# Sliding windows of a 4-D tensor: part of the input goes through the store buffers on its way in

## The chip, the cores and the metric

The kernel runs on one core of a Trainium2 chip. The metric is the device time of one execution in microseconds (us). The five engines that appear below are TensorE (PE, unused here), VectorE (DVE), ScalarE (ACT), GpSimd (POOL) and SyncE (SP). DMAs can be issued from SP, ScalarE and POOL; each of these has a DMA queue of its own (q1, q10 and q0 in the profile), and all queues are served by the same 16 DMA engines.

## The reference

The input x is 16 batches x 64 channels x 64 x 64, float32. All windows of 8 x 8 at stride 4 are copied out; nothing is computed.

```
n_h = (h - window_size) // stride + 1      # 15
n_w = (w - window_size) // stride + 1      # 15
for i in range(n_h):
    for j in range(n_w):
        result[:, i, j] = x[:, :, i*4 : i*4 + 8, j*4 : j*4 + 8]
```

The output is 16 x 15 x 15 x 64 x 8 x 8 float32, 59.0 MB; the input is 16.8 MB.

## The kernel before

The whole input is loaded once into a tile `L` of 128 partitions. The image's rows are cut into four quarters of 16 rows (`HQ`), the channels into two halves of 32 (`CH`, `CL`). Partition `ch * 64 + b * 4 + q` holds channel half `ch`, batch `b` and row quarter `q`; along the partition lie 32 channels of 16 rows of 64 numbers, so that one channel is a run of 4 KB in HBM and in `L`. The batches come in two groups of eight, `y` = 0 and 1; a group is 32 consecutive partitions in each channel half.

Loads are made by `load(eng, ch, y, q, c0, c1)`: one row quarter of the eight batches of a group, channels c0 to c1 of one half. It touches eight partitions, each four apart. The loop over y and q issues, for each pair, channels 4 to 32 of half 0 from SP (the first five pairs in two DMAs of 14 channels, the other three in one of 28), channels 0 to 4 of half 0 from POOL and channels 0 to 32 of half 1 from POOL. One DMA ahead of the loop, from ScalarE, loads channels 0 to 8 (`EC`) of half 1 for row quarter 0 and all 16 batches; POOL's loads for q = 0 leave these out. Each DMA has one of eight semaphores of its kind (eight for SP and ScalarE together, eight for POOL), so that the ninth DMA of a kind waits until the first has landed.

A store buffer is a tile `G0` to `G3` of 128 partitions x 4096 numbers; a partition holds one window of one batch with its 64 channels, 16 KB, which is one row of the output. VectorE and ScalarE fill a buffer out of `L` with copies and shuffles, and POOL writes it out with one indirect DMA (`scatter`, recorded at L131), the row numbers being in small index tiles (`idx`, `idx_y`, `idx_lo`, `idx_hi`). The last two buffers are written by SP. The four buffers are used in turn.

Three kinds of buffers follow each other. `part(y, j)` uses one batch group only: it fills four groups of 32 partitions with two window rows and two window columns, eight copies of 32 x 2048, three on ScalarE and five on VectorE (recorded at L189). `unit(j, s)` uses all batches and fills two halves of 64 partitions (L151, L154, L161, L165). The first three buffers are parts of group 0, which need only the loads of that group; then parts of group 1 alternate with units; then units alone. Two special buffers with the last window column end the program (L236).

The order of instructions on each engine is set by the framework: it schedules the program as written by the readiness of its operands, so that a ready copy can pass one that still waits for a load. It also sets all waits, from the partitions and columns of a tile that an instruction reads and writes.

Of the kernel before, what the change touches and what calls it, by code (L numbers as in the profile page):

```python
# [10 lines left out]
def kernel(  # L11
# [7 lines left out]
    nc = tc.nc  # L19
    P = nc.NUM_PARTITIONS  # L20

    B, C, H, W = x.shape
    Bo, NH, NW, Co, WSo, WSo2 = out.shape
    WS = int(window_size)
# [3 lines left out]
    f32 = mybir.dt.float32  # L28
    i32 = mybir.dt.int32
    ALU = mybir.AluOpType  # L30
    CH = 2
    HQ = P // (B * CH)
    CL = C // CH
    RB = H // HQ
# [3 lines left out]
    HP = P // CH  # L38
    YB = 8
    NY = B // YB  # L40
    QP = YB * HQ
# [4 lines left out]
    gpool = ctx.enter_context(tc.tile_pool(name="gpool", bufs=1))  # L46


    L = lpool.tile([P, CL, RB, W], f32)
# [1 line left out]

    SMALL, HWP, TWICE = 4, 8, 5

    def load(eng, ch, y, q, c0, c1):
        p0 = ch * HP + y * QP + q
        eng.dma_start(out=L[p0 : p0 + QP - HQ + 1 : HQ, c0:c1, :, :], in_=x_v[ch, y, q, :, c0:c1, :])  # L58
# [42 lines left out]
    tt(idx_lo, idx_lo, th, ALU.add)  # L101


    EC = 8
    x_b = x.rearrange("b (ch cl) (hq r) w -> ch hq b cl (r w)", ch=CH, hq=HQ)
    nc.scalar.dma_start(out=L[HP : HP + (B - 1) * HQ + 1 : HQ, 0:EC, :, :], in_=x_b[1, 0, :, 0:EC, :])

    for y in range(NY):
        for q in range(HQ):
            hw = y * HQ + q < HWP  # L110
            if hw:
                mid = (SMALL + CL) // 2 if y * HQ + q < TWICE else CL
                load(nc.sync, 0, y, q, SMALL, mid)
                if mid < CL:
                    load(nc.sync, 0, y, q, mid, CL)
            load(nc.gpsimd, 0, y, q, 0, SMALL if hw else CL)
            load(nc.gpsimd, 1, y, q, EC if q == 0 else 0, CL)

    o_v = out.rearrange("b i j c r w -> (b i j) (c r w)")
    nxt = [min(p + 1, 31) for p in range(32)]  # L120
    NG = 4
    G = [gpool.tile([P, C, WS, WS], f32, name=f"G{n}") for n in range(NG)]

    o_q = out.rearrange("b i j c r w -> i j b (c r w)")

    def free(st):
# [50 lines left out]
    def tile_():  # L177
        nonlocal at
        at += 1
        return G[(at - 1) % NG]  # L180

# [46 lines left out]
    for s in range(2):  # L228
        g = tile_()
        cols = slice(j * ST, j * ST + WS)  # L230
        for y in range(NY):
            d = slice(QP + y * QP, QP + (y + 1) * QP)
            for ch in range(CH):
                f = slice(ch * HP + y * QP, ch * HP + (y + 1) * QP)
# [39 lines left out]
```

## Time and profile before

| | |
|---|---|
| median of 3 runs | 188.5 us (188.49 to 189.4) |
| the profiled execution | 189.08 us, of which the profile's span is 187.3 us |
| VectorE, ScalarE, POOL busy | 76%, 74%, 24% of the span |
| DMA | 75.81 MB at 405 GB/s in the mean |
| HBM | 16.78 MB read, 62.91 MB written |
| POOL's queue q0 | 65.81 MB, loads and scatters |
| SP's queue q1 | 9.44 MB, 13 loads and the last two stores |
| ScalarE's queue q10 | 0.52 MB, one load |

The profile divides the span into 40 slices of 4.68 us. A DMA's share is the mean busy share of the 16 DMA engines. In the timeline a row gives the start, the time taken, the engine, the line, the operation, the tiles written and read, and in brackets how long the engine had been idle and what ended that. In part 5 of the page a copy of 32 partitions x 2048 numbers takes 1896 ns on ScalarE and 1224 ns on VectorE; the copies of L236 with 768 numbers on ScalarE take 830 ns and those with 1280 on VectorE 818 ns. A later load waits for an earlier one in the timeline as POOL's `DMA_DIRECT2D` with `DMA L<-in_x_dram` in brackets.

### The profile page before, as it was taken

The page shows a single profiled execution, that of the slowest core. Times are in us where ns is not written, and L with a number is a line of the kernel's source. Part 1 is how long each engine was busy: PE and PEld are TensorE (multiplying, and loading weights), DVE is VectorE, ACT ScalarE, POOL GpSimd, SP SyncE. Part 2 cuts the span into 40 slices and gives each one's busy share as a digit, 9 for nine tenths or more (in the row PEclk, how much of TensorE's full clock was granted, in tenths as well). Part 3 has the DMA queues.
Part 4 walks back from the last instruction along what each step waited for, and adds up shares of the span by engine and source line. Part 5 has one row for each costly group of instructions (what it writes and reads, how often), then busy time and mean ns, then how long its engine had stood idle before and what let it go on. Part 6 is the DMA issues. An engine that isn't in the chain of part 4 may idle for free.

```text
span 187.3 us, 567 instructions
## 1 busy us (share of the span) xinstructions
DVE 142.5 (76%) x203; ACT 139.3 (74%) x94; POOL 45.0 (24%) x50
## 2 busy tenths in 40 slices
DVE  5000009998597969799999999999999999999600
ACT  0000009998599979988899999998999899989700
POOL 7411222207207050501222222112211121113000
DMA  5999999999999999999999999999999999999994
GB/s 127 295 402 400 400 400 398 399 400 419 421 427 437 425 427 423 441 413 434 434 420 432 422 434 413 441 430 420 434 416 436 406 437 409 420 423 406 441 420 206
DMA packets 10988, 75.81 MB, mean 405 GB/s; under 512 B 3288, under 2 KB 3288, under 8 KB 7384
## 3 DMA queue, kind: packets, MB, share of 16 engines
q0 software_dynamic: 8784, 65.81, 84.6%
q1 hardware_dynamic: 2056, 9.44, 12.8%
q10 hardware_dynamic: 144, 0.52, 1.1%
q14 instruction: 4, 0.03, 0.0%
HBM read 16.78 MB, written 62.91 MB: 425 GB/s over the span
## 4 chain that ended last, share of the span: by engine, by line
DMA 53%; DVE 28%; issue 6%; ACT 5%; POOL 2%; ACTq 1%; DVEq 0%; PEldq 0%
DMA L<-in_x_dram 20%; DMA out_dram<-G,idx_y 14%; DVE G L161 14%; DMA out_dram<-G,idx 13%; DVE G L154 9%; DMA out_dram<-G,idx_lo 6%; DVE G L189 4%; ACT G L236 3%; POOL L L58 2%; ACT G L151 1%; ACT G L165 1%; ACTq L269 1%; DVE G L151 0%; POOL pi L69 0%; DVEq L161 0%
## 5 line engine op out<-in xcount | busy, mean ns | idle before, releaser
L151 ACT COPY G<-L 64x2048 f32<-64x2048 f32 x46 | 87.2, 1896 | 5.1 <-DMA out_dram<-G,idx 2.9
L189 DVE COPY G<-L 32x2048 f32<-32x2048 f32 x30 | 36.7, 1224 | 29.9 <-DMA L<-in_x_dram 24.1
L161 DVE STREAM_SHUFFLE G<-L 64x1024 f32<-64x1024 f32 (+4 forms) x39 | 53.0, 1360 | 1.3
L154 DVE STREAM_SHUFFLE G<-L 64x1024 f32<-64x1024 f32 x30 | 38.4, 1281 | 0.0
L189 ACT COPY G<-L 32x2048 f32<-32x2048 f32 x18 | 33.9, 1896 | 4.1 <-DMA L<-in_x_dram 2.8
L189 ACT ACT_TABLE_LOAD x1 | 1.3, 1283 | 27.7 <-DMA L<-in_x_dram 27.7
L131 POOL DMA_INDIRECT out_dram<-G,idx_y x6 | 10.0, 1664 | 28.4 <-DVE G L189 27.4
L58 POOL DMA_DIRECT2D L<-in_x_dram x16 | 11.0, 700 | 22.2 <-DMA L<-in_x_dram 21.7
L131 POOL DMA_INDIRECT out_dram<-G,idx_lo x8 | 7.7, 961 | 30.6 <-DVE G L154 26.9
L131 POOL DMA_INDIRECT out_dram<-G,idx x8 | 9.2, 1152 | 17.8 <-DVE G L161 6.8
L131 POOL DMA_INDIRECT out_dram<-G,idx_hi x7 | 6.7, 960 | 27.0 <-DVE G L154 19.0
L165 ACT COPY G<-L 64x256 f32<-64x256 f32 (+2 forms) x21 | 10.2, 484 | 0.5
L151 DVE COPY G<-L 64x2048 f32<-64x2048 f32 x6 | 7.3, 1222 | 0.2
L236 ACT COPY G<-L 32x768 f32<-32x768 f32 x8 | 6.6, 830 | 0.1
L236 DVE COPY G<-L 32x1280 f32<-32x1280 f32 x8 | 6.5, 818 | 0.1
L161 DVE LOAD_MASK_SELECT G<-L x39 | 0.3, 9 | 1.2 <-DMA out_dram<-G,idx_y 0.9
L72 DVE TENSOR_SCALAR tb<-pi 128x1 int32<-128x1 int32 x1 | 0.2, 155 | 1.0 <-POOL pi L69 1.0
L166 DVE COPY G<-L 64x1280 f32<-64x1280 f32 x1 | 0.9, 876 | 0.0
L78 DVE TENSOR_TENSOR th<-tc,tq 128x1 int32<-128x1 int32 x2 | 0.3, 156 | 0.0
L75 DVE TENSOR_SCALAR th<-tc 128x1 int32<-128x1 int32 x2 | 0.3, 154 | 0.0
L69 POOL IOTA pi<- 128x1 int32 x1 | 0.1, 124 | 0.4 <-PEq L269 0.4
L78 DVE CUSTOM_DVE_ANT_0 idx<-tb,th 128x2 uint16<-128x2 uint16 x1 | 0.2, 160 | 0.0
(19 smaller groups left out, 2.7 us busy)
## 6 DMA issues: line engine op xcount, KB each, us to landing
L<-in_x_dram POOLq DMA_DIRECT2D x6, 1024.0 KB, 21.6
L<-in_x_dram SPq DMA_DIRECT2D x10, 448.0 KB
L<-in_x_dram SPq DMA_DIRECT2D x3, 896.0 KB
out_dram<-G SPq DMA_DIRECT2D x2, 1024.0 KB
L<-in_x_dram POOLq DMA_DIRECT2D x2, 768.0 KB, 17.9
L<-in_x_dram POOLq DMA_DIRECT2D x8, 128.0 KB, 21.5
L<-in_x_dram ACTq DMA_DIRECT2D x1, 512.0 KB
out_dram<-G,idx POOLq DMA_INDIRECT x8, 12.8
```

Of the source, the lines that this page charges most:

```text
L58: eng.dma_start(out=L[p0 : p0 + QP - HQ + 1 : HQ, c0:c1, :, :], in_=x_v[ch, y, q, :, c0:c1, :])
L75: nc.vector.tensor_scalar(out=d[:, :], in0=a[:, :], scalar1=float(m), scalar2=None, op0=ALU.mult)
L78: nc.vector.tensor_tensor(out=d[:, :], in0=a[:, :], in1=b[:, :], op=op)
L131: st = nc.gpsimd.indirect_dma_start(out=o_v, out_offset=bass.IndirectOffsetOnAxis(ap=ix[:, 0:1], axis=0), in_=g.rearrange("p c r w -> p (c ...
L151: copy(out=g[d, cs, :, :], in_=L[f, :, s * ST : s * ST + WS, cols])
L154: nc.vector.stream_shuffle(out=g[d, cs, ST:WS, :], in_=L[f, :, 0:ST, cols], mask=nxt)
L161: nc.vector.stream_shuffle(out=out, in_=in_, mask=same)
L165: act(out=out[:, 0:k], in_=in_[:, 0:k])
L166: other(out=out[:, k:], in_=in_[:, k:])
L189: (act if (2 * d + ch) % 3 == 0 else dve)(out=g[d * QP : (d + 1) * QP, ch * CL : (ch + 1) * CL, :, :], in_=L[f : f + QP, :, s * ST : s * S ...
L236: copy(out=g[d, ch * CL + c0 : ch * CL + c1, :, :], in_=L[f, c0:c1, s * ST : s * ST + WS, cols])
L269: with _tile.TileContext(nc) as tc:
```

## The change

The four store buffers become slices of one tile `GG`, 128 partitions x 4 x 4096. Before the first buffer is filled, partitions 32 to 95 of that tile serve as a place to land: `S[0]` is the room of buffers 0 and 1, `S[1]` that of buffers 2 and 3, with 8 channels (`FC`) of 4 KB each. Eight DMAs, one for each row quarter and channel half, load channels 0 to 8 of that half for all 16 batches, 16 partitions to a DMA, half 0 from ScalarE and half 1 from SP. Four copies then bring them to their place in `L`, 32 partitions x 8192 numbers each: half 0 on ScalarE, half 1 on VectorE, group 0 first. They stand in the program ahead of the first part.

The other loads leave these channels out: POOL loads channels 8 to 32 of half 1, SP channels 12 to 32 and POOL channels 8 to 12 of half 0 for the first six pairs of y and q (`HWP` is 6 instead of 8); for the last two pairs POOL loads channels 8 to 32 of half 0 as well. The splitting of SP's first five loads and ScalarE's single early load are gone.

```diff
-    SMALL, HWP, TWICE = 4, 8, 5
+    SMALL, HWP = 4, 6
...
-    EC = 8
+    NG = 4
+    GF = C * WS * WS
+    GG = gpool.tile([P, NG, GF], f32)
+    G = [GG[:, n].rearrange("p (c r w) -> p c r w", c=C, r=WS) for n in range(NG)]
+    FC = NG * GF // (CH * RB * W)
+    S = [GG[:, ch * NG // CH : (ch + 1) * NG // CH].rearrange("p n f -> p (n f)").rearrange("p (c r w) -> p c r w", c=FC, r=RB) for ch in range(CH)]
+
     x_b = x.rearrange("b (ch cl) (hq r) w -> ch hq b cl (r w)", ch=CH, hq=HQ)
-    nc.scalar.dma_start(out=L[HP : HP + (B - 1) * HQ + 1 : HQ, 0:EC, :, :], in_=x_b[1, 0, :, 0:EC, :])
+    for q in range(HQ):
+        for ch in range(CH):
+            s = S[ch][QP + q : QP + q + (B - 1) * HQ + 1 : HQ]
+            (nc.scalar, nc.sync)[ch].dma_start(out=s, in_=x_b[ch, q, :, 0:FC, :])
 
     for y in range(NY):
         for q in range(HQ):
             hw = y * HQ + q < HWP
             if hw:
-                mid = (SMALL + CL) // 2 if y * HQ + q < TWICE else CL
-                load(nc.sync, 0, y, q, SMALL, mid)
-                if mid < CL:
-                    load(nc.sync, 0, y, q, mid, CL)
-            load(nc.gpsimd, 0, y, q, 0, SMALL if hw else CL)
-            load(nc.gpsimd, 1, y, q, EC if q == 0 else 0, CL)
+                load(nc.sync, 0, y, q, FC + SMALL, CL)
+            load(nc.gpsimd, 0, y, q, FC, FC + SMALL if hw else CL)
+            load(nc.gpsimd, 1, y, q, FC, CL)
+
+    for y in range(NY):
+        for ch in range(CH):
+            f = slice(QP + y * QP, QP + (y + 1) * QP)
+            d = slice(ch * HP + y * QP, ch * HP + (y + 1) * QP)
+            (nc.scalar.copy, nc.vector.tensor_copy)[ch](out=L[d, 0:FC, :, :], in_=S[ch][f])
...
-    NG = 4
-    G = [gpool.tile([P, C, WS, WS], f32, name=f"G{n}") for n in range(NG)]
```

## The prediction

> **What bounds the kernel now.** I read the page first, parts 1 to 3, to see which resource is full.
>
> ```profile
> DVE 142.5 (76%) x203; ACT 139.3 (74%) x94; POOL 45.0 (24%) x50
> ...
> DMA  5999999999999999999999999999999999999994
> GB/s 127 295 402 400 400 400 398 399 400 419 421 427 437 425 427 423 441 413 434 434 420 432 422 434 413 441 430 420 434 416 436 406 437 409 420 423 406 441 420 206
> ...
> q0 software_dynamic: 8784, 65.81, 84.6%
> q1 hardware_dynamic: 2056, 9.44, 12.8%
> q10 hardware_dynamic: 144, 0.52, 1.1%
> ```
>
> The three queues together fill 98.5% of the 16 DMA engines' span, and no compute engine is above 76%. Time can therefore come only from three places: the first two slices (4.68 us each), where 127 and 295 GB/s stand against 400; the load stage's 400 GB/s against some 425 of the stores; and a hole, if the queue ever ran dry. It never does now. Next the windows view, microsecond by microsecond, to see what the start is made of (window, its length, busy times, clock, DMA share, GB/s).
>
> ```profile
> 2.00:3.00 1.00, 0.88 (x8) 0.00 (x0) 1.00 (x3) 1.00 0.65 172
> 3.00:4.00 1.00, 0.55 (x4) 0.00 (x0) 1.00 (x2) 1.00 1.08 291
> 4.00:5.00 1.00, 0.00 (x0) 0.00 (x0) 1.00 (x3) 1.00 0.82 176
> 5.00:6.00 1.00, 0.00 (x0) 0.00 (x0) 1.00 (x3) 1.00 0.86 242
> ...
> 8.00:9.00 1.00, 0.00 (x0) 0.00 (x0) 0.29 (x1) 1.00 0.99 295
> ...
> 11.00:12.00 1.00, 0.00 (x0) 0.00 (x0) 0.00 (x0) 1.00 1.00 402
> ```
>
> There are two kinds of loss. Between 4 and 6 us the share is 0.82 and 0.86: engines are idle. At 3 and at 8 us the share is full and yet only 291 and 295 GB/s move: the packets themselves are slow. The eight rows from 2 to 10 us hold 172, 291, 176, 242, 373, 307, 295 and 332 GB/s, 2.19 MB, where 402 GB/s would have moved 3.22 MB: 2.56 us lost. Of that 0.57 us is the ramp of the first row, 0.32 us is idle engines (0.18 + 0.14), and the remaining 1.67 us is slow packets.
>
> The DMA view by window says whose packets these are.
>
> ```profile
> DMA packets 57, 0.23 MB, mean 292 GB/s; under 512 B 0, under 2 KB 0, under 8 KB 57
> ...
> q10 hardware_dynamic: 57, 0.23, 106.1%
> ```
>
> This is 3.0 to 3.8 us: ScalarE's one DMA (16 partitions, one batch each) alone on all engines, and it gets 292 GB/s. From 5 to 6 us the same view gives SP's queue, which has several 8-partition DMAs waiting, 49.3% of the engines: such a DMA uses half of them. From 30 to 32 us q0 has 57.0% and q1 47.8%: SP's loads hold one half, POOL's large loads the other.
>
> Last, the timeline of 0 to 60 us, for the moment at which stores begin.
>
> ```profile
> 27.70 1.28 ACT L189 ACT_TABLE_LOAD   x1 [27.70 <-DMA L<-in_x_dram]
> 27.77 18.64 DVE L189 COPY G<-L 32x2048 f32<-32x2048 f32 x15 [24.11 <-DMA L<-in_x_dram]
> ...
> 29.00 16.98 ACT L189 COPY G<-L 32x2048 f32<-32x2048 f32 x9
> ...
> 42.67 1.38 POOL L131 DMA_INDIRECT out_dram<-G,idx_y  x1 [8.49 <-DVE G L189]
> 44.46 2.07 POOL L131 DMA_INDIRECT out_dram<-G,idx_y  x1 [0.41 <-ACT G L189]
> 47.17 0.96 POOL L131 DMA_INDIRECT out_dram<-G,idx_y  x1 [0.65 <-issue]
> 48.78 5.74 ACT L189 COPY G<-L 32x2048 f32<-32x2048 f32 x3 [2.81 <-DMA L<-in_x_dram]
> ```
>
> ACT's nine copies take 16.98 us, 1.89 each. The seventh ends at 29.00 + 13.2 = 42.2, the eighth at 44.1, and the first two scatters follow at 42.67 and 44.46. So the copies of the first three tiles are not issued tile after tile: the first tile is complete only with ACT's seventh copy. The last load lands near 48.7 (the wait that ends at 48.78). The first scatter is issued 6 us ahead of that; this lead keeps the DMA queue full where loads pass into stores.
>
> **The change, part by part.** The sum is made against the profiled execution, 189.08 us (span 187.3 and 1.78 around it). The median of the three runs is 188.5, 0.58 lower, so I subtract that at the end.
>
> Bytes: none added. Eight DMAs of 16 partitions x 8 channels x 4 KB are 4.19 MB, SP's six of 20 channels 3.93, POOL's six of 4 channels 0.79, its ten of 24 channels 7.86: 16.78 MB, as the page reads from HBM. The new copies go through engines, not DMA. Term: 0.
>
> Halves: before, SP's half of the engines carried 7.34 MB (SP) + 1.05 (POOL's eight small loads) + 0.26, and the other half 8.13, which at 200 GB/s a half ends 2.6 us earlier, near 46 against 48.5. After the change both carry 8.39, if POOL's loads go on alternating between the halves. The mean end, about 47.2, does not move, since stores already fill the earlier half. Term: 0, as long as stores are there.
>
> Idle engines at 4 to 6 us: eight 16-partition DMAs are queued there now, so the 0.32 us goes. Term: -0.3.
>
> Issue: ScalarE issues four DMAs instead of one, SP ten instead of thirteen; one costs 0.64 to 0.7 us (0.64 on ScalarE, median 708 ns on SP). ScalarE has nothing else to do until 27.70. SP's loads are queued behind its four new DMAs, which keep its ring busy meanwhile. POOL still issues 16. Term: 0.
>
> Rate of the new stage: unknown, so bounded. The lower end is 402 GB/s from 3 us on, which gives the 1.67 us of slow packets back. The upper end is the row of the one DMA of the same shape, 292 GB/s, until all 4.19 MB are read: 14.4 us instead of 10.4, 3.9 us lost (unrounded) where 1.67 was lost before, +2.2. The shape speaks for the upper end; against it, three rings now take turns on an engine, so fewer of the 16 would read in step. I take the middle, +0.2, and keep both ends.
>
> The Trainium skill, "DMA: Bandwidth & Descriptors", section "Latency and other measured facts", says that copies whose rows lie a large power of two apart lose rate (207 GB/s at 512 KiB, 164 at 2 MiB) and suspects memory channels hit in step. The batches here are 1 MiB apart; at 207 GB/s the 4.19 MB would take 20 us, and the term would be an estimated +8. The row at 3.0 to 3.8 us leans that way but is milder; the 402 GB/s of the later loads, also 1 MiB apart with eight partitions to a DMA, contradicts it.
>
> Copies into place: 32 x 8192 each, two on ScalarE, two on VectorE. ACT: 768 elements take 830 ns and 2048 take 1896, so 0.833 ns an element and 7.0 us for 8192. DVE: 818 ns for 1280 and 1224 for 2048, 0.529 an element, 4.5 us. When can they start? An engine moves a 4 KB packet in 163 ns (402 GB/s over 16) and has 64 of the new ones, with POOL's third ring beside them. Rings take turns (SP's share falls from 49.3% to 30.9% in the microsecond after POOL's data come), so 32 turns of three take 15.6 us: SP's four, whose first packets come just before 4 us (3.0% of the engines from 2 to 4), land near 19.5, ScalarE's, started earlier, near 17.5. DVE is done at 19.5 + 8.9 = 28.4; ACT at 17.5 + 1.28 (table load, which moves here) + 14.0 = 32.8.
>
> Who waits for that? The parts (L189) need all of the first eight batches in L: 4.19 + 6.29 = 10.48 MB instead of 8.4 and some. From the 2.19 MB at 10 us, 402 GB/s reaches this at 30.6; with the following loads mixed in I take 31.5, against 27.7 before. VectorE's copies are hidden by that, ScalarE's all but 1.3 us. ACT's parts begin at 32.8 instead of 29.0, and in the old order its seventh copy ends at 46.0; the scatter's issue takes 1.38: 47.4, and the loads end at 47.2 - 0.3 = 46.9. So the lead is used up, and a hole of 0.5 us opens before any byte of the scatter moves. From the end of an issue to the first bytes ScalarE's own DMA took 0.7 us (1.38 to just after 2), POOL's first load over 1.8 (2.2 to after 4, since the DMA view of 2 to 4 us has no q0). The hole is then 0.5 to 2.3 us; I take 1.2, by the shorter of the two, since POOL is warm by then. With another order of the copies it is 0. After it nothing else is late: three tiles are then queued, 4.9 us each at 427 GB/s, until past 62, and the second group's first tile needs 6.2 us from 50.
>
> Sum: 0 + 0 - 0.3 + 0.2 + 1.2 = +1.1, 190.2 in the profiled execution, 189.6 as a median.
>
> **Rivals.** (1) The copies come tile by tile, because both channel halves now arrive together. Then the first tile is done with ACT's third copy, 32.8 + 5.7 = 38.5, no hole opens, and -0.3 + 0.2 gives 188.4. For it: the old order fits one half arriving much later, and POOL's share of the early loads shrinks. Against: nothing shows that order. (2) The new loads run at 402 GB/s at once and land some 2 us earlier, so ACT is ready with the data: -0.3 - 1.7, 186.5. For it: all later loads run so. Against: the 292 row. (3) The new loads keep 292 GB/s until they have landed, because 16 rows 1 MiB apart are read in step. The copies then start some 3 us later, the parts near 36, the first scatter's issue ends near 50.6, loads at 49.1, so the hole is 1.5 + 0.7: -0.3 + 2.2 + 2.2, 192.6. It decides once the stage's mean stays under about 330 GB/s. For it: the 292 row. Against: the 16 engines drift apart as POOL's packets come between. This is the rule of the Trainium skill named above, at the milder price of this trace. (4) The one tile of all store buffers makes every fill wait for every store, as if it were one buffer: 31 tiles with some 3 us or more uncovered each, over 280 us. L, also one tile, is read at 27.77 while other rows are still loaded until 48.7, so parts of a tile are told apart; I give it 2%.
>
> **How the numbers follow.** The forecast (a hole of 0.5 to 2.3 us, rate near the middle, 188.9 to 190.7) has 0.32, rival 1 0.26, rival 2 0.19, rival 3 0.21, rival 4 0.02. About 0.5%, 0.94 us, is what a measurement of this kernel can tell from no change: faster is below 187.56, slower above 189.44. Faster: 0.19 + 0.04 of rival 1. Same: 0.22 of rival 1 and 0.12 of the forecast. Slower: 0.20 + 0.21 + 0.02. The range goes from just above rival 2's time to a little short of rival 3's, leaving about a tenth out at each side: 186.6 to 192.2. The forecast's own range is 188.9 to 190.7.
>
> **What would show it.** In the changed profile: the GB/s of 3 to 18 us (near 400: rival 2; near 290: rival 3); two ACT copies of 32x8192 at 7.0 us ending near 32.8 and DVE's at 4.5 ending near 28.4; the first DMA_INDIRECT near 46 (or near 38.5: rival 1); a dip below 400 GB/s between 46 and 49. A first scatter before 43 and no dip would make the forecast wrong, as would a load stage that ends more than 1.5 us from 47.

## The result: a gain in the loads, lost again in two places

The changed kernel takes 189.69 us (median of 5 runs, 189.54 to 189.88), the kernel before 188.56 (5 runs, 188.49 to 189.4). The ratio is 1.0047 [1.0035, 1.006]: slower by half a per cent. The profiled executions differ by 0.8 us: 189.88 us with a span of 188.1 against 189.08 with 187.3.

The page of the changed kernel, parts 1 to 3:

```profile
DVE 151.1 (80%) x205; ACT 153.3 (81%) x96; POOL 52.1 (28%) x50
...
DMA  5999999998999999999999999999999999999995
GB/s 166 385 410 403 400 398 399 386 387 348 390 446 408 423 432 408 436 418 418 427 402 432 432 411 425 418 418 439 394 439 413 422 425 415 425 429 408 439 418 230
...
q0 software_dynamic: 8656, 65.55, 84.5%
q1 hardware_dynamic: 1744, 8.13, 10.8%
q10 hardware_dynamic: 576, 2.10, 3.0%
```

The bytes are the same. The first two slices move more (166 and 385 GB/s; 127 and 295 before). New is a dip in the tenth slice (42 to 47 us): an 8 in the DMA row and 348 GB/s. The later slices hide a third difference, too small to see by eye.

The windows view of the changed kernel (window, length, busy times of DVE, ACT and POOL, clock, DMA share, GB/s):

```profile
3.00:4.00 1.00, 0.53 (x4) 0.00 (x0) 1.00 (x2) 1.00 1.00 344
4.00:5.00 1.00, 0.00 (x0) 0.00 (x0) 1.00 (x3) 1.00 1.07 422
5.00:6.00 1.00, 0.00 (x0) 0.00 (x0) 1.00 (x3) 1.00 0.89 291
6.00:7.00 1.00, 0.00 (x0) 0.00 (x0) 0.37 (x1) 1.00 1.00 393
7.00:8.00 1.00, 0.00 (x0) 0.00 (x0) 0.00 (x0) 1.00 1.05 422
8.00:9.00 1.00, 0.00 (x0) 0.00 (x0) 0.25 (x1) 1.00 1.02 410
9.00:10.00 1.00, 0.00 (x0) 0.00 (x0) 0.30 (x1) 1.00 1.02 410
...
11.00:12.00 1.00, 0.00 (x0) 0.00 (x0) 0.00 (x0) 1.00 1.04 414
```

The new loads run at full rate nearly at once: 422 GB/s at 4 us and 410 at 8, where the kernel before had 176 and 295. After the ramp before 4 us only the row at 5 us still loses much. In wider windows, first the kernel before, then the changed one:

```profile
2.00:10.00 8.00, 1.43 (x11) 0.00 (x0) 5.02 (x9) 1.00 0.91 273
...
44.00:46.00 2.00, 1.99 (x2) 1.98 (x2) 1.58 (x2) 1.00 1.09 440
...
50.00:66.00 16.00, 14.73 (x14) 15.73 (x9) 4.82 (x3) 1.00 1.01 430
```

```profile
2.00:10.00 8.00, 1.43 (x11) 0.00 (x0) 4.92 (x9) 1.00 0.97 354
...
44.00:46.00 2.00, 1.94 (x3) 1.98 (x2) 1.58 (x1) 1.00 0.58 207
46.00:48.00 2.00, 1.94 (x3) 1.98 (x2) 0.51 (x1) 1.00 0.94 393
48.00:50.00 2.00, 1.99 (x2) 1.98 (x2) 1.32 (x1) 1.00 1.21 516
50.00:66.00 16.00, 15.63 (x14) 15.78 (x10) 5.41 (x3) 1.00 0.98 410
```

From 2 to 10 us 81 GB/s more for 8 us are 0.65 MB gained. From 44 to 46 us the share is 0.58: a hole.

To add this up I spread each packet's bytes evenly over its time and sum over all packets (a window's own figure moves by up to 0.2 MB with the packets that straddle its ends). The changed kernel has then moved this much more than the kernel before: +0.65 MB at 10 us, +0.55 at 44, +0.15 at 48, -0.02 at 66, -0.43 at 180. At 425 GB/s the gain of 0.55 MB is 1.3 us. The hole takes 0.40 MB between 44 and 48 us (0.9 us), the slow start of the stores up to 66 us another 0.17 MB (0.4 us). The long store stage, from 66 us on, takes another 0.41 MB (1.0 us). The net is 1.0 us; the spans differ by 0.8.

The timeline of the changed kernel shows why the hole opens:

```profile
17.67 1.28 ACT L129 ACT_TABLE_LOAD   x1 [17.67 <-DMA GG<-in_x_dram]
18.17 8.87 DVE L129 COPY L<-GG 32x8192 f32<-32x8192 f32 x2 [14.54 <-DMA GG<-in_x_dram]
18.66 10.95 POOL L58 DMA_DIRECT2D L<-in_x_dram  x6 [9.36 <-DMA L<-in_x_dram]
18.96 14.06 ACT L129 COPY L<-GG 32x8192 f32<-32x8192 f32 x2
30.21 1.22 DVE L198 COPY GG<-L 32x2048 f32<-32x2048 f32 x1 [3.17 <-DMA L<-in_x_dram]
...
33.05 22.89 ACT L198 COPY GG<-L 32x2048 f32<-32x2048 f32 x12
33.05 23.61 DVE L198 COPY GG<-L 32x2048 f32<-32x2048 f32 x19 [1.62 <-ACT L L129]
43.82 1.76 POOL L140 DMA_INDIRECT out_dram<-GG,idx_y  x1 [11.65 <-DVE GG L198]
47.49 1.83 POOL L140 DMA_INDIRECT out_dram<-GG,idx_y  x1 [1.92 <-DVE GG L198]
51.20 1.83 POOL L140 DMA_INDIRECT out_dram<-GG,idx_y  x1 [1.88 <-DVE GG L198]
```

ScalarE's copies into place end at 33.0 us. The parts begin then, on VectorE too: it has made one part copy and then waits 1.62 us for ScalarE. By the program only part copies into partitions 64 to 95 of the first two store buffers need ScalarE's second copy, because its landed channels of group 1 still lie there; the trace does not name the partitions that this part copy writes. The first scatter is issued at 43.82, takes 1.76 and moves its first 16 KB packet at 46.1; the last 4 KB packet of a load ended at 45.6. The kernel before had its first scatter at 42.67 and its last load packet at 48.1.

The store stage, in the DMA view from 66 to 170 us, before and after:

```profile
DMA packets 3281, 44.21 MB, mean 425 GB/s; under 512 B 581, under 2 KB 581, under 8 KB 581
```

```profile
DMA packets 3267, 43.94 MB, mean 422 GB/s; under 512 B 584, under 2 KB 584, under 8 KB 584
```

Summed packet by packet it is 425.7 against 421.6 GB/s, in a stage in which the change adds and removes no instruction.

### The profile page after: what moved, and what is told of

Its sections match the earlier page's. It is cut to its first block, busy times and chain, and to the rows that moved or that the text cites. A ratio compares the mean times of both kernels' runs of the same rounds, so it can differ in the third digit from the quotient of the medians.

```text
span 188.1 us, 577 instructions
## 1 busy us (share of the span) xinstructions
DVE 151.1 (80%) x205; ACT 153.3 (81%) x96; POOL 52.1 (28%) x50
## 2 busy tenths in 40 slices
DMA packets 10980, 75.81 MB, mean 403 GB/s; under 512 B 3280, under 2 KB 3280, under 8 KB 7376
## 3 DMA queue, kind: packets, MB, share of 16 engines
HBM read 16.78 MB, written 62.91 MB: 424 GB/s over the span
## 4 chain that ended last, share of the span: by engine, by line
DVE 39%; DMA 35%; ACT 9%; issue 8%; POOL 2%; ACTq 1%; DVEq 0%; PEldq 0%
DVE GG L170 14%; DVE GG L198 14%; DMA out_dram<-GG,idx 13%; DMA L<-in_x_dram 11%; DVE GG L163 10%; DMA out_dram<-GG,idx_y 6%; DMA out_dram<-GG,idx_lo 5%; ACT L L129 4%; ACT GG L245 3%; POOL L L58 2%; DVE GG L160 1%; ACT GG L160 1%; ACT GG L174 1%; ACTq L278 0%; DVEq L198 0%
## 5 line engine op out<-in xcount | busy, mean ns | idle before, releaser
L160 ACT COPY GG<-L 64x2048 f32<-64x2048 f32 x46 | 87.1, 1896 | 5.2 <-DMA out_dram<-GG,idx 3.5
L170 DVE STREAM_SHUFFLE GG<-L 64x1024 f32<-64x1024 f32 (+4 forms) x39 | 52.9, 1357 | 1.3
L198 DVE COPY GG<-L 32x2048 f32<-32x2048 f32 x30 | 36.6, 1219 | 5.5 <-DMA L<-in_x_dram 3.2
L163 DVE STREAM_SHUFFLE GG<-L 64x1024 f32<-64x1024 f32 x30 | 38.5, 1282 | 0.0
L198 ACT COPY GG<-L 32x2048 f32<-32x2048 f32 x18 | 34.0, 1896 | 0.4
L129 DVE COPY L<-GG 32x8192 f32<-32x8192 f32 x2 | 8.8, 4418 | 14.6 <-DMA GG<-in_x_dram 14.5
L140 POOL DMA_INDIRECT out_dram<-GG,idx_y x6 | 10.5, 1753 | 27.9 <-DVE GG L198 19.9
L140 POOL DMA_INDIRECT out_dram<-GG,idx x8 | 9.8, 1229 | 21.4 <-ACT GG L160 8.1
L129 ACT ACT_TABLE_LOAD x1 | 1.3, 1283 | 17.7 <-DMA GG<-in_x_dram 17.7
L129 ACT COPY L<-GG 32x8192 f32<-32x8192 f32 x2 | 14.0, 7017 | 0.0
L174 ACT COPY GG<-L 64x256 f32<-64x256 f32 (+2 forms) x21 | 10.2, 484 | 0.5
```

The source lines that it names most:

```text
L129: (nc.scalar.copy, nc.vector.tensor_copy)[ch](out=L[d, 0:FC, :, :], in_=S[ch][f])
L140: st = nc.gpsimd.indirect_dma_start(out=o_v, out_offset=bass.IndirectOffsetOnAxis(ap=ix[:, 0:1], axis=0), in_=g.rearrange("p c r w -> p (c ...
L160: copy(out=g[d, cs, :, :], in_=L[f, :, s * ST : s * ST + WS, cols])
L163: nc.vector.stream_shuffle(out=g[d, cs, ST:WS, :], in_=L[f, :, 0:ST, cols], mask=nxt)
L170: nc.vector.stream_shuffle(out=out, in_=in_, mask=same)
L174: act(out=out[:, 0:k], in_=in_[:, 0:k])
```

## Experiments

Two things had to be explained. For the slower store stage:

- Theory A: it runs at some 425 GB/s when the two halves of the DMA engines enter it some us apart, and at some 421 when they enter in step. In the kernel before, the 16 semaphore updates with which the first store reports its landing come in two groups, seven from 50.05 to 50.65 us and eight from 53.01 to 53.52, with one at 52.10 between them. In the changed kernel, where both halves carry 8.39 MB, all 16 come from 51.46 to 51.62.
- Rivals: it is chance (B), or the one tile of all store buffers does it (F).

For the fast new loads:

- Theory D: what counts is where a DMA writes. Rows that all lie in one half of the 128 partitions (0 to 63, or 64 to 127) are written at a low rate by 16 engines; rows on both sides of 64 are not.
- Rival E: what counts is what it reads, 16 rows 1 MiB apart (rival 3 of the prediction).

For all rows on the halves below, their distance is the mean of the last eight of a store's 16 semaphore updates less the mean of the first eight, as the median over the stores that land between 60 and 170 us. The trace does not name the engine of an update, so the two groups are told apart by time alone.

**Both kernels once more.** No edit.

> The kernel before once more, for the spread of its trace. Theory A (stores run slower in the changed kernel because all 16 DMA engines enter the store stage in step after a hole): the stage from 66 to 170 us moves 425 GB/s again, within 0.5. Rival B (that difference is chance from one execution to the next): this run differs from 425 by 2 or more, as the changed kernel's 422 did. First scatter at 42.7 us under both.

> The changed kernel once more. Theory A: 422 GB/s from 66 to 170 us again, a window from 44 to 46 us at about 207 GB/s, first scatter at 43.8. Rival B: the rate from 66 to 170 us lies anywhere between 421 and 426.

Measured: 188.82 us and 425.9 GB/s from 66 to 170 us; 189.73 us and 421.4 GB/s. The hole is there again (244 GB/s from 44 to 46 us), and so is the fast start (278 and 353 GB/s from 2 to 10 us). Chance falls.

**ScalarE's second copy shared with VectorE.**

```diff
+            if y == 1 and ch == 0:
+                nc.scalar.copy(out=L[d, 0 : FC // 2, :, :], in_=S[ch][f, 0 : FC // 2])
+                nc.vector.tensor_copy(out=L[d, FC // 2 : FC, :, :], in_=S[ch][f, FC // 2 : FC])
+                continue
```

> The changed kernel, with ScalarE's second copy (half 0, second batch group) shared: four of its eight channels on VectorE. By the rows of the changed kernel ScalarE is then done at 18.96 + 7.0 + 3.5 = 29.5 instead of 33.0, VectorE at 18.17 + 4.4 + 2.3 + 4.4 = 29.3, so the first tiles are filled from 30.2 (when the loads allow it) and the first scatter comes at about 41.6 instead of 43.8. Theory A (the hole costs 1.0 us, stores in step cost over 1 us): the hole at 44 to 46 us closes and the time falls by about 1.0 to 188.7 us; the stores stay near 422 GB/s if the engines still end the loads together, and gain up to 1 us more if they do not. Rival C (the copies cost by their work on the two engines, the hole is not what matters): no change, 189.5 to 189.9.

Measured: 188.24 us (187.98 to 188.28), ratio to the kernel before 0.9966 [0.9952, 0.9979], 1.45 us less than the changed kernel. Windows:

```profile
44.00:46.00 2.00, 1.97 (x2) 1.98 (x2) 0.16 (x1) 1.00 1.16 457
...
50.00:66.00 16.00, 15.63 (x14) 15.80 (x9) 6.55 (x4) 1.00 1.01 429
```

The copies into place end at 29.4 us instead of 33.0 and the first scatter comes at 42.16 instead of 43.82. That closes the hole (457 GB/s) and the slow start after it (429). At 66 us this kernel is 0.60 MB ahead of the changed one, 1.4 us, which is the whole gain in time; 1.0 us was expected, for the hole alone. The store stage stays at 422.0 GB/s. So ScalarE's 14.06 us of copies cause the hole, and not the slower stores.

**No landing place.** The eight DMAs write straight into `L`; the four copies go.

```diff
-            s = S[ch][QP + q : QP + q + (B - 1) * HQ + 1 : HQ]
+            s = L[ch * HP + q : ch * HP + q + (B - 1) * HQ + 1 : HQ, 0:FC, :, :]
...
-    for y in range(NY):
-        for ch in range(CH):
-            f = slice(QP + y * QP, QP + (y + 1) * QP)
-            d = slice(ch * HP + y * QP, ch * HP + (y + 1) * QP)
-            (nc.scalar.copy, nc.vector.tensor_copy)[ch](out=L[d, 0:FC, :, :], in_=S[ch][f])
```

> The changed kernel without the detour: the same eight DMAs of 16 partitions write straight into their place in the large input tile, that is into one half of the partitions each, and the four copies are left out. All other loads as in the changed kernel. Theory D (the early rate of the kernel before, 292 GB/s, came from 16 engines writing into one half of the 128 partitions; the changed kernel's destination straddles both halves): the rate from 3 to 10 us falls from the changed kernel's 400 to 290 to 370 GB/s, as ScalarE's go to one half and SP's to the other. Rival E (it came from reading rows 1 MiB apart, and passed for another reason): the rate is that of the changed kernel, since the addresses read are the same. For the time: without copies the tiles start when the loads allow it, about 30, the first scatter is at about 41.5, no hole; 187.8 to 188.8 us under both, less under E.

**The landing place in partitions 0 to 63 instead of 32 to 95.**

```diff
-            s = S[ch][QP + q : QP + q + (B - 1) * HQ + 1 : HQ]
+            s = S[ch][q : q + (B - 1) * HQ + 1 : HQ]
...
-            f = slice(QP + y * QP, QP + (y + 1) * QP)
+            f = slice(y * QP, (y + 1) * QP)
```

> The changed kernel with the landing place in partitions 0 to 63 instead of 32 to 95; the copies read from there. Same addresses read, same DMAs. Theory D (16 engines that write into one half of the partitions get a lower rate): the rate from 2 to 10 us falls from 354 to 240 or less, since now both queues write into the same half, the landing ends some 6 us later or more, and the time rises by at least 3 us, to 193 or more. Rival E (the reading decides): 354 GB/s and 189.7 us stay.

Measured: without the landing place 193.56 us (193.39 to 193.61), ratio 1.0249 [1.0235, 1.0263]; with it in partitions 0 to 63, 199.73 us in one run, against 188.79 of the kernel before beside it. Windows of the two, in this order:

```profile
2.00:10.00 8.00, 1.42 (x11) 0.00 (x0) 4.38 (x8) 1.00 0.96 240
10.00:18.00 8.00, 0.00 (x0) 0.00 (x0) 0.55 (x1) 1.00 1.04 305
```

```profile
2.00:10.00 8.00, 1.43 (x11) 0.00 (x0) 4.37 (x8) 1.00 0.98 210
10.00:18.00 8.00, 0.00 (x0) 0.00 (x0) 0.55 (x1) 1.00 1.05 244
18.00:30.00 12.00, 3.18 (x1) 3.68 (x2) 2.71 (x1) 1.00 1.03 300
```

The same queues read the same rows; the partitions written differ (and without the landing place the copies are gone too), and the rate falls from 354 GB/s to 240 and 210 at a full DMA share. Rival E falls and theory D stands. Without the landing place two expected figures were missed: the rate fell further than the 290 to 370 GB/s foreseen, and so the time came out at 193.56 us instead of 187.8 to 188.8. Two queues that write one half each do not make up for it (240); that they hit the same half at the same moments would explain this, but was not shown. The Trainium skill, "SBUF — State Buffer", section "Door 1: The DMA port swizzle (why `[64,N]` ≈ `[32,N]`)", says that partitions 0 to 63 share eight of 16 ports, with 196 GB/s measured for 1 MiB. This case agrees: 210 to 244 GB/s from 2 to 18 us, with the other loads of that time counted in, and the landing place from 32 to 95, which reaches both halves, gets 393 to 422 from 6 to 10 us. That page of the Trainium skill, section "Can I just issue two DMAs to hit both halves?", tells of two DMAs, one on each half, that moved only 6% more than one; here it is 240 against 210 GB/s from 2 to 10 us, 14% more, with two queues in both cases.

**The one tile alone.** The kernel before, with its four store buffers as slices of one tile.

```diff
-    G = [gpool.tile([P, C, WS, WS], f32, name=f"G{n}") for n in range(NG)]
+    GG = gpool.tile([P, NG, C * WS * WS], f32)
+    G = [GG[:, n].rearrange("p (c r w) -> p c r w", c=C, r=WS) for n in range(NG)]
```

> The kernel before with its four store buffers as slices of one tile and nothing else. Theory A: 425 to 426 GB/s from 66 to 170 us, as before, time 188.8. Rival F (the one tile slows the stores): 421 to 423 GB/s, about 189.8.

Measured: 188.91 us, against 188.79 of the kernel before; stores at 425.7 GB/s. Neither the time nor the store rate comes from the one tile. F falls, and with it the prediction's rival 4.

**The halves set apart.** To the shared copies, one load moved from POOL to SP at the end.

```diff
-            load(nc.gpsimd, 1, y, q, FC, CL)
+            last = y * HQ + q == NY * HQ - 1
+            if last:
+                load(nc.sync, 1, y, q, CL - 8, CL)
+            load(nc.gpsimd, 1, y, q, FC, CL - 8 if last else CL)
```

> The shared-copies kernel with one more edit: the last eight channels of half 1 for the last pair of y and q are loaded by SP, not POOL, so that SP's half of the engines has 16 packets of 4 KB more to move than the other and ends the loads about 2.6 us later, as in the kernel before. Bytes and copies are the same. Theory A (stores run at 421 instead of 425 GB/s where both halves of the DMA engines enter the store stage together): the rate from 66 to 170 us goes back to 425 or 426 and the time falls by 0.8 to 1.0 us, to about 187.3. Rival F (the rate belongs to the one tile of all buffers, or to the order of the copies): 421 GB/s and 188.2 us stay.

Measured: 189.49 us (189.24 to 189.53), ratio 1.0029 [1.002, 1.0039]. The store rate is back at 425.4 GB/s with the halves 2.0 us apart, as theory A has it. The time is a miss: from 30 to 42 us the rate fell to 354 GB/s (391 with the shared copies alone), and at 44 us 0.53 MB, 1.25 us, are missing. The moved load makes SP's engines write the same half as POOL's; by theory D that costs rate, which fits, but was not tried by itself.

**The halves of the kernel before brought together.** The last of SP's loads is cut by nine channels, which POOL loads.

```diff
+                last = y * HQ + q == NY * HQ - 1
...
-                load(nc.sync, 0, y, q, SMALL, mid)
+                load(nc.sync, 0, y, q, SMALL, mid - 9 if last else mid)
...
+            if y * HQ + q == NY * HQ - 1:
+                load(nc.gpsimd, 0, y, q, CL - 9, CL - 8)
+                load(nc.gpsimd, 0, y, q, CL - 8, CL)
```

> The kernel before, with the halves of the DMA engines made to end the loads together: for the last pair of y and q, SP loads nine channels less, and POOL loads them in two more DMAs, of one channel and of eight, of which the second falls to the other half of the engines. Each half then moves 256 packets of 4 KB an engine instead of 264 and 248. Theory A: the stores from 66 to 170 us fall from 425 to 421 or 422 GB/s and the time rises by 0.8 to 1.2 us, to about 189.8. Rival F: 425 GB/s and 188.8 us stay, or a little less than 188.8.

Measured: 189.03 us (188.72 to 189.36), ratio 1.0008 [0.9998, 1.0017]. The edit missed its aim: the halves stayed 2.2 us apart, and the stores at 425.6 GB/s. As a trial of bringing them together it says nothing on theory A.

**Unequal landing.** Fewer channels of one half go through the landing place, so that a half of the engines carries more: `FCS` is (6, 8), (7, 8) and (4, 8) on the changed kernel, and (8, 6) on the one with the shared copies.

```diff
+    FCS = (6, 8)
...
-            (nc.scalar, nc.sync)[ch].dma_start(out=s, in_=x_b[ch, q, :, 0:FC, :])
+            n = FCS[ch]
+            (nc.scalar, nc.sync)[ch].dma_start(out=s[:, 0:n], in_=x_b[ch, q, :, 0:n, :])
...
-                load(nc.sync, 0, y, q, FC + SMALL, CL)
-            load(nc.gpsimd, 0, y, q, FC, FC + SMALL if hw else CL)
-            load(nc.gpsimd, 1, y, q, FC, CL)
+                load(nc.sync, 0, y, q, FCS[0] + SMALL, CL)
+            load(nc.gpsimd, 0, y, q, FCS[0], FCS[0] + SMALL if hw else CL)
+            load(nc.gpsimd, 1, y, q, FCS[1], CL)
...
-            (nc.scalar.copy, nc.vector.tensor_copy)[ch](out=L[d, 0:FC, :, :], in_=S[ch][f])
+            (nc.scalar.copy, nc.vector.tensor_copy)[ch](out=L[d, 0 : FCS[ch], :, :], in_=S[ch][f, 0 : FCS[ch]])
```

> The changed kernel, with six channels of half 0 (ScalarE's) in the landing place instead of eight; the two channels more go with GpSimd's loads of half 0. So the engines that write half 0 get more bytes than the others, by 16 packets of 4 KB, and the two halves should again enter the store stage about 2.6 us apart, as in the kernel before. ScalarE's two copies shrink from 7.0 to about 5.3 us each and end near 29.5 us. Theory A (stores run at 425 GB/s when the halves enter the store stage apart, at 421 to 422 when they enter together): 425 to 426 GB/s between 66 and 170 us; first scatter near 42 us, no hole at 44 to 46 us; about 187.3 us. Rival (the store rate depends on something else that the landing brought, such as code or placement): 421 to 422 GB/s, about 188.2 us.

> Seven channels of half 0 in the landing place, eight of half 1: the halves should enter the store stage about 1.3 us apart, and ScalarE's copies end near 31.2 us. Theory A: between the two states, 422 to 425 GB/s between 66 and 170 us, a small hole or none at 44 to 46 us, 187.6 to 188.6 us. Rival: 421 to 422 GB/s, about 188.6 us.

> Four channels of half 0 in the landing place, eight of half 1: the halves should enter the store stage about 5.2 us apart, and ScalarE's copies end near 26 us. Theory A: 425 GB/s if any distance does; 421 if about one whole store of distance (4.9 us) counts as together again; 187.2 to 188.2 us. The load stage itself ends later on one half, which may cost up to 1 us. Rival: 421 to 422 GB/s, 188.2 us or more.

> The kernel in which VectorE takes half of ScalarE's second copy, with eight channels of half 0 and six of half 1 in the landing place: the halves should enter the store stage about 2.6 us apart, half 1's engines the later ones. Theory A: 425 GB/s between 66 and 170 us, no hole, about 187.3 us. Rival: 421 to 422 GB/s, about 188.2 us.

Measured, beside the kernel before at 188.77 us (188.61 to 188.92, 13 runs):

| | time, us | ratio | first scatter, us |
|---|---|---|---|
| (6, 8) | 187.67 (187.64 to 187.78) | 0.9941 [0.9928, 0.9955] | 39.88 |
| (7, 8) | 187.13 (187.08 to 187.28) | 0.9913 [0.9899, 0.9926] | 37.44 |
| (4, 8) | 189.47 (189.04 to 189.61) | 1.0033 [1.0022, 1.0044] | 43.33 |
| (8, 6), shared | 188.19 (188.07 to 188.34) | 0.9969 [0.9958, 0.998] | 42.30 |

The kernel with (7, 8) beats both. Its windows, and its stores in the DMA view from 66 to 170 us:

```profile
44.00:46.00 2.00, 1.94 (x3) 1.98 (x2) 1.43 (x1) 1.00 1.10 449
...
50.00:66.00 16.00, 15.61 (x14) 15.80 (x9) 6.55 (x4) 1.00 1.00 429
```

```profile
DMA packets 3288, 44.26 MB, mean 426 GB/s; under 512 B 585, under 2 KB 585, under 8 KB 585
```

It keeps the fast start (355 GB/s from 2 to 10 us), has no hole, and its stores run as before the change. At 180 us it has moved 1.04 MB more than the changed kernel, 2.4 us; the times differ by 2.56.

Over all 14 profiles, those of the prediction included, the store rate from 66 to 170 us rises with the distance of the halves, up to some 1.5 us:

| kernel | distance, us | GB/s |
|---|---|---|
| landing in 0 to 63 | 0.40 | 421.3 |
| changed, twice | 0.44, 0.44 | 421.6, 421.4 |
| shared copies | 0.51 | 422.0 |
| no landing place | 0.61 | 422.1 |
| (8, 6), shared | 0.75 | 423.6 |
| (4, 8) | 1.26 | 424.3 |
| (7, 8) | 1.41 | 425.2 |
| (6, 8) | 1.76 | 425.4 |
| before, twice | 1.98, 2.09 | 425.7, 425.9 |
| halves set apart | 2.00 | 425.4 |
| one tile alone | 2.04 | 425.7 |
| before, attempt to bring together | 2.23 | 425.6 |

Theory A stands as a dependence: six profiles with less than 1 us between the halves, of five ways of loading, lie under 424 GB/s, and eight with more lie over it. The rival of the last four expectations, 421 to 422 everywhere, falls. Yet the distance is itself measured in the store stage, and the edits did not always set it as intended, so that distance sets the rate is argued, not shown; why engines in step store 1% slower is open. Nor is it the whole of it: summed from 66 to 135 us the rates spread from 421.4 to 427.7 GB/s, while from 135 to 170 us all 14 profiles lie between 420.7 and 422.5, the kernel before too, with 1.3 us between its halves. What holds the rate down there was not looked into.

Of the four expected times only that of (6, 8), about 187.3 us, was near. With (7, 8) the kernel was faster than the 187.6 to 188.6 us foreseen. With (8, 6) the distance came out at 0.75 us instead of 2.6, so most of the gain stayed away. With (4, 8) it came out at 1.26 us instead of 5.2, and the lighter half runs out of loads near 42 us, before the first scatter at 43.33:

```profile
42.00:44.00 2.00, 1.94 (x3) 1.95 (x3) 0.67 (x1) 1.00 0.54 199
44.00:46.00 2.00, 1.97 (x2) 1.89 (x1) 1.33 (x2) 1.00 0.67 276
```

The share of 0.54 is what half of the engines idle would give; by 48 us 0.66 MB (1.5 us) are lost against (7, 8). With (6, 8) 0.14 MB are lost against (7, 8) between 50 and 66 us (419 GB/s), where the halves, 3.4 us apart, come closer again.

The first scatter moves between 37.44 and 43.82 us with the order in which the framework sets the part copies. Before it come five on ScalarE and nine on VectorE in the changed kernel, seven and eleven with (4, 8), but three and five with (7, 8): the first buffer is then filled alone, the order of rival 1. Why the framework chooses so was not worked out. The timeline of (7, 8):

```profile
30.16 23.04 ACT L200 COPY GG<-L 32x2048 f32<-32x2048 f32 x12 [1.13 <-DMA L<-in_x_dram]
30.38 24.90 DVE L200 COPY GG<-L 32x2048 f32<-32x2048 f32 x20 [4.00 <-DMA L<-in_x_dram]
...
37.44 1.75 POOL L142 DMA_INDIRECT out_dram<-GG,idx_y  x1 [5.62 <-DVE GG L200]
```

## Why the prediction was right, and where it was not

Forecast 189.6, measured 189.69. That the sum met the time so closely is luck: a gain that was sized too small and a loss that was not in it nearly cancel. The prediction's own signs say the same. The first scatter came after 43 us and the loads ended 1.45 us from 47, both just inside what it allowed, but the 396 GB/s from 3 to 18 us are rival 2's sign.

- **Bytes, issue.** Right: 16.78 MB read, 75.81 moved. SP's and ScalarE's issues cost nothing visible.
- **Idle engines (-0.3) and rate (+0.2).** Mis-sized: together -0.1, measured 0.65 MB by 10 us, -1.5. The new stage came near rival 2, though not at once: 354 GB/s from 2 to 10 us, with the ramp and the row at 5 us. The step that failed was taking the row of ScalarE's one DMA at 292 GB/s as that of "the one DMA of the same shape". It had 16 partitions as the new ones have, but all in one half; the direct and the low-half runs show that this makes the rate. The middle of two bounds was taken where one of them belonged to another case. The rule on row pitch of the Trainium skill ("DMA: Bandwidth & Descriptors", "Latency and other measured facts") did not decide here: the same 1 MiB apart, the rows were read at 393 to 422 GB/s from 6 to 10 us. The estimate of +8 also misread that row of the Trainium skill: its copies run between HBM tensors and reach 214 GB/s at what it calls full rate, so 207 at 512 KiB is a loss of 3% there, not a rate to set against a load at 402.
- **Copies.** Right. Part 5 of the page of the changed kernel:

```profile
L129 DVE COPY L<-GG 32x8192 f32<-32x8192 f32 x2 | 8.8, 4418 | 14.6 <-DMA GG<-in_x_dram 14.5
...
L129 ACT COPY L<-GG 32x8192 f32<-32x8192 f32 x2 | 14.0, 7017 | 0.0
```

  Foreseen were 4.5 and 7.0 us, ends at 28.4 and 32.8; measured 4.42 and 7.02, 27.0 and 33.0. The landings came at 17.7 and 18.2 (17.5 and 19.5 foreseen), and the parts at 33.05 (32.8), where they wait for ScalarE as foreseen, VectorE by a wait that the prediction did not name (by the program, on the landed data in the store buffers).
- **First scatter.** Near 46 foreseen, in the old order; it came at 43.82, with VectorE's ninth part copy. The order changed in part, not to rival 1's 38.5.
- **Hole.** 1.2 us foreseen, 0.9 measured, with both ends earlier: the loads ended at 45.6 instead of 46.9, because of the faster start. (The 46.9 left out the sum's own +0.2 for the rate; with it the foreseen hole is 1.0.) "After it nothing else is late" was too good: stores then come one at a time, 50 to 66 us run at 410 GB/s, and up to 66 us another 0.4 us is lost.
- **Halves (0).** The term that failed. Both halves carry the same, as foreseen, and the prediction saw a cost only in a hole. The stores then ran at 421.6 instead of 425.7 GB/s, which cost 1.0 us; by theory A because the halves store in step.
- **Rivals.** Rival 2 had the rate nearly right and the hole wrong. Rival 3's mechanism is refuted by the direct run, rival 4's by the one tile alone. With (7, 8) the first scatter comes at 37.44, no hole opens and the stores keep their rate: 187.13, the fast start turned into time. Rival 1's order is what that kernel has.

## What to carry to other kernels

A DMA's shape is its rows and the partitions that it writes: before a rate is borrowed from a row of the profile, see in which half of the 128 partitions both land. When a load stage gets faster, ask whether the first store can be ready that much earlier, since otherwise the gain comes back as a hole at the seam; here 3.6 us less of an engine's copies were worth 1.4 us of time. And sum the bytes moved at several times in both kernels: it showed a loss of 1% in the one stage that the change didn't touch.

## What the runs showed that was not expected

- The store stage runs 1% slower in the kernels in which the two halves of the DMA engines work in step (421 to 422 GB/s from 66 to 170 us under 0.65 us of distance, 425 from 1.4 us on).
- With full DMA shares (0.96 and 0.98), 240 and 210 GB/s moved: a share of 1 says that the engines hold packets, not that they move them at full rate.
- Two of POOL's load issues took 4.35 and 4.15 us beside VectorE's copies into place, where the others took 0.55 to 0.75. The Trainium skill, "SBUF — State Buffer", section "🔬 SBUF: two separate sides", describes this: POOL can't write descriptors while VectorE makes such a copy. The durations agree, with 4.42 us for each of these copies; no starved DMA engine followed, the DMA share being 1.04 from 18 to 30 us.
